# A hybrid decoder layer on one core: attention interleaved without emptying points, deeper load leads, later area returns, block sums ahead

## The chip, the cores and the metric

The kernel runs on one core of a Trainium2 chip. The metric is the device time of one execution in microseconds (us). Engines: PE is TensorE (matrix products), DVE is VectorE, ACT is ScalarE, POOL is GpSimd, and SP is the engine that here only issues DMAs. All engines share the on-chip memory and synchronise by semaphores; each works through its own instructions strictly in order.

## The reference, cut to what matters

One layer of a decoder with 512 positions and model width 2048. Two attentions read columns of one input projection, two sigmoid gates from the same projection weigh them, then come a cross attention to 256 memory tokens and an MLP. All in float32.

```python
def reference(x, mem, g_mix, w_in, ...):
    xn = rmsnorm(h, g_mix[l])
    (q_a, k_c, v_c, k_s, v_s, k_w, v_w, g_nsa, c_q, c_kv, k_r,
     gate_a, gate_b) = jnp.split(xn @ w_in[l], bounds, axis=-1)
    ...
    o_a = nsa_attention(q_a, kc, vc, ks, vs, kw, vw, g_nsa, ...)
    o_b = mla_attention(c_q, c_kv, k_r, mla_g_q[l], mla_w_uq[l], mla_g_kv[l],
                        mla_w_uk[l], mla_w_uv[l], cos_b, sin_b)
    mixed = (jax.nn.sigmoid(gate_a) * (o_a @ w_o_nsa[l])
             + jax.nn.sigmoid(gate_b) * (o_b @ w_o_mla[l]))
    h = h + mixed @ w_out[l]
    h = h + memory_cross_attention(rmsnorm(h, g_xattn[l]), rmsnorm(mem, g_mem[l]),
                                   xa_wq[l], xa_wkv[l], xa_wo[l])
    hn = rmsnorm(h, g_mlp[l])
    h = h + jnp.square(jax.nn.relu(hn @ w_ff1[l])) @ w_ff2[l]
return rmsnorm(h, g_final)
```

NSA has 16 heads of width 96 with three branches (compressed, selected, window); MLA has 16 heads, whose queries come from a latent of rank 512 (`w_uq`), and keys and values from one of rank 256 (`w_uk`, `w_uv`).

## The kernel before, in words

**Values.** Every float32 operand is held as a high part and a low remainder, `HL`. A product takes three matmuls (`mm`, L513 to L515: high by high, high by low, low by high). The split costs an ACT copy (`hr`, L526, L335, L1789, L1865) and a DVE subtraction (`lr`, L527, L347, L1794, L1870).

**Stages.** The program is a chain of projections, in this order: P0 to P6 (the input projection's columns for NSA), M0 and M1 (`proj_m`: columns for MLA's latents and `w_o`'s input), mk0, mk1, mv (`mem_k`, `mem_v`: the memory's keys and values), then `mla()`: uq (`mla_q`, MLA's queries, four heads for each q of 0 to 3), ukv (`mla_kv`, keys and values of the same heads), mk2 and mk3, and wn (`wn`, four column blocks of `w_o_nsa`). Then g0 to g3 (`Gates.run`: both gates' columns in four blocks, each in 7 products of a Strassen-like scheme, so 28 passes), wm (`w_o_mla`), `w_out`, the cross attention and the MLP. Up to wn most go through `chunk`, which calls `on_k(k)` and one step of the generator `bg` at each k step.

**Attention beside.** Attention doesn't have stages of its own. `Side` holds a queue of generators. After each product of a stage `side.run(rate / 4, ...)` emits so many attention steps: score matmuls (L513 to L515 into `st`), a softmax with DVE maximum and ACT exponential (L701, L702) and DVE scaling (L720), transposes of the probabilities (L799), their ACT and DVE splits (L543, L544) and the product with the values (L818, L820). The rates stand in the table `T`, by stage: r0 to r2 for P and M, rk for mk and mv, ru for uq, rw for ukv and wn, rt for the gates. A stage's `post` generator, also run beside later stages, transposes its heads (`heads_T`, L648); q's and K's heads are first turned by the rope, on POOL (`rope`, L632 to L635). `side.drain()` runs the queue empty at one place. It is called at the end of mv (all of NSA), after mk3, and after ukv1, ukv2 and ukv3 (MLA's heads of one q each).

**What sets the order.** All orders are written out by hand: an instruction stands in its engine's queue where the program emits it. There is no scheduler.

**Memory.** On-chip memory is a pool of 40 areas of 128x1024 words (`slots`, printed `s`) and five pairs (`d`); `get` takes an area and `put` gives it back. Whoever takes a returned area waits, on the chip, until its last reader is done.

**Weights.** `Stream` and, in the gates, `load`, `high`, `low` (`prep`) bring them: SP issues plain loads, POOL issues loads that add to an area (L1784). `prep(i)` runs AHEAD = 3 steps before the product.

**Blocks written to memory and read again.** NSA's and MLA's output goes block by block to `d_nsa` and `d_mla`; `load_o` reads it back and splits it (L526). It holds two halves of areas: it issues block j, then splits block j − 1. `mem_load` does the same for the memory's 16 half blocks in M1, two per k from k = 5. `Gates.fetch` loads x (`xT`, 16 blocks of 256 KB on SP) and multiplies each block by its gain on ACT (L2215, two instructions for each), two k steps per k of wn3, into the eight areas `A`.

**Block sums.** Of a column block's 7 products, n = 1 to 4 multiply a sum of A's blocks. `stat` makes the sum on POOL (`add`, L1838 to L1844) and its high part on ACT (L1865), `stat_low` the low one on DVE (L1870); for c = 0 in the pass before its use, later blocks use it again. `use` takes a finished product: into a sum area for n < 3; from n = 3 on it ends one output block: ACT's Tanh (L2306), a DVE product with the NSA branch for the first two column blocks (L2311), a store to `d_g` by ACT's queue (L2313), and `put`.

## Time and profile before

| | us |
|---|---|
| median of 3 runs | 2884.34 (2883.65 to 2887.16) |
| the profiled execution's own time | 2884.04 |
| its span in the trace | 2882.2 |
| mean granted TensorE clock | 0.988 of full speed |

The stages, by the first matmul of each in the trace (us from the start of the span):

| stage | start | stage | start | stage | start |
|---|---|---|---|---|---|
| P6 | 341.3 | mk3 | 652.2 | wn2 | 794.8 |
| M0 | 412.9 | uq1 | 660.0 | ukv3 | 828.7 |
| M1 | 475.8 | wn0 | 676.6 | wn3 | 843.2 |
| mk0 | 554.3 | ukv1 | 712.9 | g0 | 886.0 |
| mv | 574.7 | uq2 | 722.8 | g1 | 1000.4 |
| uq0 | 619.3 | wn1 | 734.8 | g2 | 1092.2 |
| mk2 | 635.3 | ukv2 | 768.7 | g3 | 1168.4 |
| ukv0 | 646.6 | uq3 | 782.8 | wm | 1254.0 |

How to read the profile's rows: `635.32 0.58 PE L513 MATMUL mm<-s,s ... [7.56 <-ACT s L1284]` is an instruction that started at 635.32 us and took 0.58, of line 513 on PE; it writes a tile of the name `mm` and reads two areas `s`; the engine had stood idle for 7.56 us, and what ended that was ACT's instruction of line 1284 on an area. A row of the waits, `ACT s L1789 <- DMA d_g<-s: 23.5, 6, 9.2`, is an instruction group, what it waited for, the us in total, the number of waits and the longest. A row of the windows gives a stretch of time, its length, each engine's busy time with the number of instructions, the granted TensorE clock, the mean busy share of the DMA engines and GB/s.

### The profile page before, as it was taken

Reading aid. Unit: us, or ns where it says so; the run is one execution under the profiler, and the core shown is the slowest. Engines: PE = TensorE matmul, PEld = TensorE weight load, DVE = VectorE, ACT = ScalarE, POOL = GpSimd, SP = SyncE. Lnnn points to the kernel's source line nnn. Section 1 sums busy time; section 2 is a strip of 40 time slices with the busy share of each in tenths; the row PEclk is TensorE's granted clock in tenths of the full one; section 3 lists DMA queues with packets and bytes.
Section 4 is the critical chain, followed back from the end, with each engine's and each line's share of the span. In section 5 each row is a group of like instructions: output and inputs, shape, how many; then the busy total and the mean of one; then the engine's idle time right before and its main releaser. Section 6 shows DMA issues by size and latency. Waiting matters only on the chain.

```text
span 2882.2 us, 38227 instructions
## 1 busy us (share of the span) xinstructions
PE 2794.2 (97%) x13974; PEld 2365.4 (82%) x13974; DVE 2020.2 (70%) x3179; ACT 1648.9 (57%) x2746; POOL 483.7 (17%) x698
## 2 busy tenths in 40 slices
PE   9999999889987989999999999999999999999998
PEld 7888889878876768778998888888888888888887
DVE  6347677766655667645786677777776788888888
ACT  5445556656665556643465866666666654444445
POOL 3130110111112211100230111111111111111110
PEclk9999999999998999999999999999999999999999
DMA  5322112233236888867862799888898889999996
GB/s 180 97 87 67 57 63 68 80 106 99 78 120 161 231 207 210 213 213 217 185 140 81 214 240 220 205 218 211 211 219 206 208 229 227 233 236 231 241 226 175
DMA packets 165357, 497.95 MB, mean 173 GB/s; under 512 B 17072, under 2 KB 34352, under 8 KB 165168
## 3 DMA queue, kind: packets, MB, share of 16 engines
q0 software_dynamic: 50688, 184.57, 34.1%
q1 hardware_dynamic: 85088, 271.44, 27.6%
q10 hardware_dynamic: 29392, 39.50, 3.9%
q8 instruction: 109, 1.79, 0.3%
q14 instruction: 80, 0.66, 0.1%
HBM read 453.50 MB, written 41.94 MB: 172 GB/s over the span
## 4 chain that ended last, share of the span: by engine, by line
PE 57%; DMA 3%; DVE 3%; issue 3%; ACT 1%; POOL 1%; ACTq 0%; DVEq 0%; POOLq 0%; SPq 0%
PE mm L1976 9%; PE mm L1977 9%; PE mm L1975 9%; PE st L1977 5%; PE st L1975 5%; PE st L1976 5%; PE mm L513 2%; PE mm L514 2%; PE mm L515 2%; DMA d_g<-s 1%; PE mm L1565 1%; PE mm L1563 1%; PE mm L1564 1%; DVE s L1794 1%; PE mm L2053 1%
## 5 line engine op out<-in xcount | busy, mean ns | idle before, releaser
L1975 PE MATMUL mm<-s,s 128*128 128x512 f32 x1472 | 579.7, 394 | 13.6 <-ACT s L1789 10.7
L1976 PE MATMUL mm<-s,s 128*128 128x512 f32 x1472 | 577.9, 393 | 7.7 <-DVE s L1794 7.7
L1977 PE MATMUL mm<-s,s 128*128 128x512 f32 x1472 | 577.6, 392 | 3.2 <-DVE s L1870 3.2
L1794 DVE TENSOR_TENSOR s<-s,s 128x1024 fp32r<-128x1024 f32 x316 | 383.3, 1221 | 201.8 <-ACT s L1789 196.4
L1789 ACT CAST s<-s 128x1024 fp32r<-128x1024 f32 x316 | 327.2, 1049 | 184.7 <-DMA s<-wts 129.0
L513 PE MATMUL mm<-s,s 128*128 128x512 f32 (+5 forms) x1012 | 400.4, 396 | 13.9 <-ACT s L1284 11.8
L515 PE MATMUL mm<-s,s 128*128 128x512 f32 (+5 forms) x1012 | 384.0, 379 | 0.7 <-DVE s L530 0.6
L514 PE MATMUL mm<-s,s 128*128 128x512 f32 (+5 forms) x1012 | 383.3, 379 | 0.0
L347 DVE TENSOR_TENSOR s<-s,s 128x512 fp32r<-128x512 f32 (+4 forms) x408 | 284.1, 714 | 81.8 <-ACT s L335 81.3
L1975 PEld LDWEIGHTS mm<-s,s 128*128 128x128 f32 x1472 | 279.3, 190 | 71.8 <-ACT s L1789 11.9
L1976 PEld LDWEIGHTS mm<-s,s 128*128 128x128 f32 x1472 | 279.0, 190 | 67.5 <-DVE s L1794 10.9
L1977 PEld LDWEIGHTS mm<-s,s 128*128 128x128 f32 x1472 | 279.0, 190 | 63.5 <-DVE s L1870 5.5
L335 ACT CAST s<-s 128x512 fp32r<-128x512 f32 (+4 forms) x408 | 241.4, 604 | 147.8 <-PE mm L515 44.5
L1784 POOL DMA_DIRECT2D s<-wts x167 | 145.9, 875 | 734.2 <-DVE s L1794 420.3
L1975 PE MATMUL st<-s,s 128*128 128x512 f32 x676 | 264.2, 391 | 0.0
L1977 PE MATMUL st<-s,s 128*128 128x512 f32 x676 | 262.8, 389 | 0.0
L1976 PE MATMUL st<-s,s 128*128 128x512 f32 x676 | 262.5, 388 | 0.0
L1789 ACT CAST s<-d 128x1024 fp32r<-128x1024 f32 x159 | 165.1, 1048 | 167.3 <-DMA d<-wts 155.4
L1794 DVE TENSOR_TENSOR s<-d,s 128x1024 fp32r<-128x1024 f32 x159 | 193.2, 1220 | 53.9 <-ACT s L1789 53.0
L513 PEld LDWEIGHTS mm<-s,s 128*128 128x128 f32 x1012 | 192.5, 190 | 39.0 <-ACT s L1284 12.4
L515 PEld LDWEIGHTS mm<-s,s 128*128 128x128 f32 x1012 | 192.0, 190 | 34.3 <-DVE s L530 2.0
L702 ACT ACTIVATE PP<-PP,mx 128x512 f32<-128x512 f32 (+2 forms) x208 | 116.1, 558 | 171.1 <-DVE mx L701 170.3
(399 smaller groups left out, 5152.2 us busy)
## 6 DMA issues: line engine op xcount, KB each, us to landing
s<-wts SPq DMA_DIRECT2D x280, 512.0 KB, 4.9
s<-wts POOLq DMA_DIRECT2D x199, 512.0 KB, 8.3
d<-wts POOLq DMA_DIRECT2D x101, 512.0 KB, 8.6
d<-wts SPq DMA_DIRECT2D x58, 512.0 KB, 7.5
PP<-wts POOLq DMA_DIRECT2D x52, 512.0 KB, 8.6
PP<-wts SPq DMA_DIRECT2D x33, 512.0 KB, 8.4
d_u<-s ACTq DMA_DIRECT2D x64, 256.0 KB, 5.3
s<-xT SPq DMA_DIRECT2D x47, 256.0 KB, 4.1
```

Of the source, the lines that this page charges most:

```text
L335: self.k.nc.scalar.copy(o.hr, self.at[n][:, s])
L347: self.k.nc.vector.tensor_sub(o.lr, t[:, s], o.hi)
L513: t.matmul(ps, a.hr, b.hr, start=first, stop=False)
L514: t.matmul(ps, a.hr, b.lr, start=False, stop=False)
L515: t.matmul(ps, a.lr, b.hr, start=False, stop=last)
L702: self.later("x", 1, lambda: nc.scalar.activation(p, p, AF.Exp, bias=mx, scale=-1.0, accum_out=sm))
L1784: self.nc.gpsimd.dma_start(t, src, accum_op=OP.add)
L1789: self.nc.scalar.copy(t.hr, self.raw[i])
L1794: self.nc.vector.tensor_sub(t.lr, r, t.hi)
L1975: m(ps, a.hr, b.hr, start=first, stop=False, skip_group_check=True)
L1976: m(ps, a.hr, b.lr, start=False, stop=False, skip_group_check=True)
L1977: m(ps, a.lr, b.hr, start=False, stop=last, skip_group_check=True)
```

## The change

It has five parts.

1. `mla()` no longer drains. Attention's generators are put into the queue when their heads are ready (by ukv's `post`), and run on through the stages until they are done, within the gates. The order of the stages becomes uq(q), ukv(q), wn(q − 1). `d_nsa` is read back in uq1 and ukv1 and no longer in uq0 and uq1. The rates change to match, with rv for ukv0 and r3 for uq1 and ukv1 added.
2. `load_o` has four halves, and loads three steps ahead of the split; it waits until a block's store has been emitted. `mem_load` has the same lead, and runs one half block per k through all of M1.
3. `fetch` loads x by eight DMAs of 512 KB, straight into `A`, and POOL multiplies in place by the gain.
4. `presum(n)` makes the sum of n on POOL a pass earlier than `stat` did; `stat` only splits it.
5. `use` doesn't give the area of a `d_g` store back at once but after the next pass's products (`done`).

TensorE's attention and head-transposing instructions beside each stage, by the order of the program before and of the changed one:

| | M0 | M1 | mv | uq0 | mk2 | ukv0 | mk3 | uq1 | wn0 | ukv1 | uq2 | wn1 | ukv2 | uq3 | wn2 | ukv3 | wn3 | g0 |
|---|---|---|---|---|---|---|---|---|---|---|---|---|---|---|---|---|---|---|
| before | 192 | 188 | 117 | 0 | 16 | 0 | 18 | 18 | 93 | 23 | 26 | 83 | 43 | 26 | 83 | 43 | 69 | 69 |
| changed | 149 | 150 | 115 | 18 | 43 | 14 | 37 | 21 | 97 | 25 | 27 | 97 | 30 | 27 | 97 | 28 | 85 | 50 |

The core of the diff:

```diff
-T = dict(pace=0.75, r0=3.7, r1=4.05, r2=4.0, rk=1.1, ru=2.6, rw=3.4, rt=0.8)
+T = dict(pace=0.75, r0=3.7, r1=4.05, r2=3.0, rk=1.15, ru=2.9, rv=3.7, r3=2.6, rw=3.9, rt=0.9)
...
         def on_k(k):
             if k:
                 self.put(self.X[k - 1])
-            if k > 4:
-                for _ in range(2):
-                    next(ml, None)
+            next(ml, None)
...
     def mla_kv(self, q, qs, rate):
...
-        self.side.post = self.heads_T(4, out.append)
-        return out, vs
+        def post():
+            yield from self.heads_T(4, out.append)
+            self.side.add(self.attend(self.mla_items(q, qs, out, vs)))
+            if q == 3:
+                self.side.add(self.flush())
+        self.side.post = post()
...
     def mla(self):
...
-        self.side.drain()
...
+        qs = self.mla_q(0, T["ru"])
+        self.mem_k(2, T["rk"])
+        self.mla_kv(0, qs, T["rv"])
+        self.mem_k(3, T["rk"])
...
-            if q < 3:
-                self.wn(q, T["rw"])
-                ks, vs = self.mla_kv(q + 1, T["rw"])
-                self.side.drain()
+        self.bg = self.load_o(self.d_nsa, self.N)
+        for q in range(1, 4):
+            qs = self.mla_q(q, T["ru"] if q > 1 else T["r3"])
+            self.mla_kv(q, qs, T["rw"] if q > 1 else T["r3"])
+            if q == 1:
+                drain(self.bg)
+                self.bg = None
+            elif q == 2:
+                self.mem_scale()
+            self.wn(q - 1, T["rw"])
...
+    def load_o(self, dram, out, lag=3):
+        while len(self.slots.free) < 2:
             yield
+        st, sl = self.halves(4)
+        for j in range(8 + lag):
+            if j < 8:
+                while (id(dram), j) not in self.stored:
+                    yield
+                self.nc.sync.dma_start(st[j % 4], dram[j])
+            if j >= lag:
+                while not self.slots.free:
+                    yield
+                out.append(self.slot_hl())
+                self.split(out[-1], st[(j - lag) % 4])
+            yield
...
     def fetch(self):
...
+                self.A[t, h] = [k.slots.plain() for _ in range(2)]
+                for i in range(2):
+                    d = 8 * h + 4 * i
+                    nc.sync.dma_start(self.A[t, h][i].rearrange("p (k n) -> p k n", k=4),
+                                      k.a["xT"][d:d + 4, :, 256 * t:256 * t + 256].rearrange("k p n -> p k n"))
+        for h in range(2):
+            for t in range(2):
+                yield
+                for i in range(2):
+                    d = G_MIX + 8 * h + 4 * i
+                    x = self.A[t, h][i].rearrange("p (k n) -> p k n", k=4)
+                    nc.gpsimd.tensor_mul(x, x, k.gains[:, d:d + 4][:, :, None].to_broadcast([128, 4, 256]))
+        self.presum(1)
+
+    def presum(self, n):
+        if n > 4:
+            return
+        self.m = self.sums.get(n - 1)
+        self.sums[n] = [self.k.slots.plain() for _ in range(2)]
+        for h in range(2):
+            self.add(n, h, self.sums[n][h])
...
     def run(self, rate):
...
             self.before(c, n)
+            if p < 4:
+                self.presum(p + 2)
...
-            self.use(c, n, ps)
+            while self.done and self.done[0][0] < p:
+                k.put(self.done.popleft()[1])
+            self.use(p, c, n, ps)
...
         nc.scalar.dma_start(self.rows(self.k.d_g, blk, c), o.rearrange("p (t n) -> p t n", t=2))
-        self.k.put(o)
+        self.done.append((p, o))
```

The same in three engines' orders. The first is TensorE's queue in ukv2, where `mm<-s_99` and `mm<-s_97` are ukv's products, L648 or L649 the head transposes into `st`, and L799 or L800 attention's transposes. Before, in the drain behind ukv2:

```order
L515 MATMUL mm<-s_99,d_5423 128x512
L648 MATMUL st<-cst,s_153 96x128 x2
L648 MATMUL st<-cst,s_154 96x128 x2
L799 MATMUL st<-cst,PP 128x128 x4
L818 MATMUL o<-s_1687,d_6825 128x128
```

Changed, in the middle of ukv2:

```order
L516 MATMUL mm<-s_97,s_5223 128x512
L800 MATMUL st<-cst,PP 128x128 x3
L649 MATMUL st<-cst,s_153 96x128 x2
L649 MATMUL st<-cst,s_154 96x128 x2
L514 MATMUL mm<-s_97,s_5248 128x512
```

The pair of L648 or L649 rows stands four times in a row in both (it is shown once). Before they were K's heads of ukv2 behind its last product; now they are the queries of uq2, between ukv2's products, and K's heads follow in wn.

The second is POOL's queue from wn3 to the first gate products: L1307 copies MLA's rope columns, L1784 or L1793 are the loads of weights that add, L2233 the multiplications by the gain, and the L1838 to L1840 or L1847 to L1849 the block sums. Before:

```order
L1307 COPY s_154<-s_154 128x4x32 x2
L1784 DMA s_8393<-wts 128x1024
L1784 DMA s_8395<-wts 128x1024
L1784 DMA s_8404<-wts 128x1024
L1784 DMA s_8406<-wts 128x1024
L1838 TENSOR_TENSOR s_8488<-d_8115,d_8117 128x1024
L1784 DMA s_8393<-wts 128x1024
L1784 DMA s_8395<-wts 128x1024
L1838 TENSOR_TENSOR s_8489<-d_8115,d_8117 128x1024
```

Changed:

```order
L1307 COPY s_154<-s_154 128x4x32 x2
L2233 TENSOR_TENSOR s_8139<-s_8139,gains 128x1024
L2233 TENSOR_TENSOR s_8140<-s_8140,gains 128x1024
L2233 TENSOR_TENSOR s_8143<-s_8143,gains 128x1024
L2233 TENSOR_TENSOR s_8144<-s_8144,gains 128x1024
L2233 TENSOR_TENSOR d_8125<-d_8125,gains 128x1024 x2
L2233 TENSOR_TENSOR d_8126<-d_8126,gains 128x1024 x2
L1847 TENSOR_TENSOR s_8327<-s_8143,d_8126 128x1024
L1847 TENSOR_TENSOR s_8328<-s_8144,d_8126 128x1024
L1793 DMA s_8360<-wts 128x1024
L1793 DMA s_8362<-wts 128x1024
L1849 TENSOR_TENSOR s_8486<-s_8327,s_8139 128x1024
```

Eight multiplications and the first sum's two halves now stand ahead of the first adding load.

The third is ACT's queue in the first gate block, behind an output block's store. Names are areas with their uses numbered: L1789 or L1798 takes weights' high parts, L1865 or L1877 the sums'. Before:

```order
L2313 DMA d_g_89<-s26_8875 128x2x512
L1789 CAST s9_8965<-d4_8771 128x1024
L1865 CAST s10_8971<-d1_8116 128x1024
L1789 CAST s26_8986<-PP_105 128x1024
L1789 CAST s8_9004<-PP_105 128x1024
```

Changed:

```order
L2346 DMA d_g_89<-s3_8763 128x2x512
L1798 CAST s16_9018<-s32_8360 128x1024
L1877 CAST s8_9023<-d0_8126 128x1024
L1798 CAST s34_9038<-s33_8362 128x1024
L1798 CAST s12_9057<-d1_8127 128x1024
L1877 CAST s28_9063<-d0_8126 128x1024
L1798 CAST s38_9078<-d1_8127 128x1024
L2339 ACTIVATE s36_8667<-s36_8667,hrx_8128 128x512 x2
L2346 DMA d_g_89<-s36_8667 128x2x512
L1798 CAST s6_9103<-s15_9042 128x1024
L1877 CAST s14_9108<-s24_8139 128x1024
L1798 CAST s3_9123<-s31_9061 128x1024
```

Before, the third row behind the store writes into the area that the store reads (`s26`); now it is the eleventh (`s3`), a pass later.

## The prediction, made before the changed kernel was run

> **What bounds the kernel now.** I read the busy shares and the chain of waits of the page first.

> ```profile
> PE 2794.2 (97%) x13974; PEld 2365.4 (82%) x13974; DVE 2020.2 (70%) x3179; ACT 1648.9 (57%) x2746; POOL 483.7 (17%) x698
> PE 57%; DMA 3%; DVE 3%; issue 3%; ACT 1%; POOL 1%; ACTq 0%; DVEq 0%; POOLq 0%; SPq 0%
> ```

> TensorE is busy for 97% of the 2882.2 us span and holds 57% of the chain; no other engine is near its limit over the whole. The change adds and removes practically no matmul, so it can only win where TensorE stands still or runs at a lower granted clock. The next view cuts the span by stage (the table ahead of this prediction names them) and asks each stretch for busy time and granted clock.

> ```profile
> core 0: us, PE busy (x) PEld busy (x) DVE busy (x) ACT busy (x) POOL busy (x), PEclk, DMA share, GB/s
> 412.90:475.80 62.90, 61.61 (x386) 58.27 (x385) 47.51 (x159) 37.52 (x108) 9.69 (x32) 1.00 0.20 61
> 475.80:554.30 78.50, 69.74 (x381) 62.44 (x379) 57.20 (x180) 52.30 (x157) 11.53 (x15) 0.93 0.25 78
> 574.70:619.30 44.60, 41.40 (x216) 33.09 (x215) 32.65 (x95) 25.30 (x67) 0.00 (x0) 1.00 0.34 106
> 619.30:646.60 27.30, 18.12 (x113) 17.36 (x112) 10.40 (x20) 11.71 (x21) 7.14 (x16) 0.87 0.36 126
> 660.00:676.60 16.60, 12.05 (x69) 10.96 (x67) 10.31 (x27) 11.67 (x26) 0.00 (x0) 1.00 0.42 140
> 676.60:712.90 36.30, 36.30 (x189) 30.93 (x190) 24.98 (x66) 20.41 (x48) 8.45 (x20) 0.95 0.20 63
> 734.80:768.70 33.90, 33.90 (x180) 28.70 (x180) 21.04 (x55) 17.83 (x43) 6.99 (x19) 1.00 0.22 70
> 768.70:782.80 14.10, 12.28 (x68) 9.36 (x68) 8.72 (x25) 10.26 (x25) 0.00 (x0) 1.00 0.36 113
> 828.70:843.20 14.50, 12.36 (x69) 9.40 (x68) 9.16 (x25) 10.58 (x25) 0.00 (x0) 1.00 0.39 110
> 843.20:886.00 42.80, 34.43 (x166) 28.02 (x164) 22.19 (x60) 30.64 (x72) 1.01 (x1) 0.95 0.57 179
> 886.00:1000.40 114.40, 97.24 (x405) 78.48 (x406) 71.42 (x88) 56.41 (x79) 33.15 (x24) 0.88 0.80 206
> 1000.40:1092.20 91.80, 81.44 (x337) 64.49 (x336) 59.19 (x54) 52.58 (x60) 13.97 (x17) 0.94 0.83 212
> 1092.20:1168.40 76.20, 76.20 (x338) 63.07 (x337) 57.02 (x52) 51.08 (x58) 15.75 (x19) 1.00 0.86 198
> 1168.40:1254.00 85.60, 79.41 (x337) 63.84 (x336) 53.40 (x54) 50.55 (x62) 11.19 (x13) 0.98 0.84 212
> ```

> I call **loss** a stage's length less its PE busy time, plus length times the missing clock. For g0: 114.4 − 97.24 + 0.12 × 114.4 = 30.9 us. So worked out, the others are M0 1.3, M1 14.3, mv 3.2, uq0 with mk2 12.7, uq1 4.6, wn0 1.8, ukv2 1.8, ukv3 2.1, wn3 10.5, g1 15.9, g3 7.9; wn1 and g2 lose nothing. The sum is 107 us: removing every loss would give 2884.04 − 107 = 2777 us. The gates g0 to g3 hold 54.7 of it. The table of waits and single rows of the timeline tell what these losses are made of.

> ```profile
> ACT s L1789 <- DMA d_g<-s: 23.5, 6, 9.2
> POOL s L1784 <- DVE s L1794: 152.5, 18, 52.8
> ACT s L1865 <- POOL s L1838: 7.0, 2, 4.2
> ACT s L526 <- DMA s<-d_mla: 14.5, 5, 5.4
> 635.32 0.58 PE L513 MATMUL mm<-s,s 128*128 128x256 f32 x1 [7.56 <-ACT s L1284]
> 779.50 0.64 PE L648 MATMUL st<-cst,s 128*96 128x128 f32 x4 [0.52 <-DVE s L544]
> 849.85 0.51 ACT L2215 ACTIVATE s<-s,gains 128x256 f32<-128x256 f32 x1 [5.35 <-DMA s<-xT]
> 854.47 0.58 PE L513 MATMUL st<-s,s 96*128 96x256 f32 x1 [5.11 <-DVE s L544]
> 895.48 1.04 ACT L1865 CAST s<-s 128x1024 fp32r<-128x1024 f32 x1 [4.19 <-POOL s L1838]
> 898.14 0.48 PE L513 MATMUL st<-s,s 96*128 96x128 f32 x1 [4.77 <-DVE s L544]
> 976.80 1.99 ACT L1789 CAST s<-PP 128x1024 fp32r<-128x1024 f32 x2 [8.56 <-DMA d_g<-s]
> 977.90 0.79 PE L1975 MATMUL mm<-s,s 128*128 128x512 f32 x1 [4.59 <-ACT s L1789]
> 1068.31 1.04 ACT L1789 CAST s<-s 128x1024 fp32r<-128x1024 f32 x1 [9.25 <-DMA d_g<-s]
> ```

> A bracket holds the idle time before the row, and what ended it. Everywhere the same pattern: ScalarE stands at the head of its order before something that has only just been started (an area that a store is still reading, a load issued a moment ago, a sum that GpSimd is still making), and TensorE behind it runs dry some microseconds later.

> **The change part by part.** All terms are against the profiled execution's own 2884.04 us, of which 2882.2 is span; the median of the runs, 2884.34, is 0.3 us from it, so that no correction is needed.

> *M0 and M1.* TensorE's attention matmuls beside them fall from 192 and 188 to 149 and 150, and the memory's blocks are converted one step per k and not two, three blocks behind their loads. M0 lost 1.3 us with 192, so density alone doesn't stall; M1's loss comes with the doubled ACT work (52.3 us against 37.5). Of 15.6 I take **10**, bounds 4 and 14.

> *mv, uq0 and mk2.* The drain at the end of mv goes, and the 7.56 us before mk2 (ACT converting d_nsa blocks straight after their loads) has attention beside it, with d_nsa moved away. The square root's chain stays. Of 15.9 I take **10**, bounds 4 and 14.

> *uq1 and wn0.* uq1 waited for evacuations behind d_nsa's second half, now spread over uq1 and ukv1. Of 6.4 I take **3.4**, bounds 0 and 6.

> *ukv1 to ukv3.* A drain after each goes (at most 5 us with ukv1), and a wait comes. q's head transposes stood at the end of wn; now they stand in the middle of ukv right behind uq, and need GpSimd's rope, which runs then.

> ```profile
> 794.19 0.49 POOL L632 TENSOR_TENSOR rp<-s,cst 128x128 f32<-128x128 f32 x1 [26.99 <-ACT s L1284]
> 800.21 0.79 POOL L635 TENSOR_TENSOR s<-rp,rp 128x128 f32<-128x128 f32 x1
> ```

> From first to last rope it is 6.8 us, ending 6.2 us after uq3's end at 794.8. ukv's matmuls ahead of the transposes cover some 4 us. At 2 us for each of three places against 5 gained: **−1**, bounds −14 (three waits of 6.2 and the 5) and +5. Behind a waiting transpose stand ukv's own matmuls, on which K's heads wait.

> *wn3 and the fetch.* x's 16 loads of 256 KB and 32 ACT activations become 8 loads of 512 KB and 8 GpSimd multiplies of 128x1024 plus two sums. ACT's 5.35 us wait and the 5.11 us of TensorE that followed go. GpSimd's price comes from the sums of the same shape:

> ```profile
> 892.76 2.69 POOL L1838 TENSOR_TENSOR s<-d,d 128x1024 f32<-128x1024 f32 x1
> 903.31 0.29 DVE L720 TENSOR_SCALAR PP<-PP,r 128x128 f32<-128x128 f32 x1
> 922.83 2.99 DVE L720 TENSOR_SCALAR PP<-PP,r 128x128 f32<-128x128 f32 x1
> 923.08 2.64 POOL L1842 TENSOR_TENSOR s<-s,d 128x1024 f32<-128x1024 f32 x1
> ```

> Ten times 2.69 is 26.9 us of GpSimd, beside weights' loads that it also issues. And it isn't free to VectorE: a 128x128 scaling that elsewhere takes 0.29 us took 2.99 at 922.83 and ended with GpSimd's sum. [...] By the rows, VectorE is busy 22.2 us in 42.8 here, so most instructions find a gap between two of GpSimd's. I take **+2.5** of 10.5; bounds −16.4 (all 26.9 on the path in place of 10.5) and +8.

> *g0 and g1.* Two edits. The area of a d_g store goes back a pass later, so ACT no longer writes into one being read: that wait was 8.56 us before 976.80 and 9.25 before 1068.31, with 4.59 of TensorE idle behind the first. And GpSimd's sums are made a pass ahead: 4.19 before 895.48, 4.77 of TensorE. Of g0's 30.9 I give the stores 8.5 and the sums 18.6 at 60%, 11, less 4 that transfers take back: **15.5**, bounds 5 and 27. Of g1's 15.9, 14 is stores; less 6 taken back: **8**, bounds −8 and 15. What is late next is the loads:

> ```profile
> DMA packets 25468, 76.25 MB, mean 207 GB/s; under 512 B 2423, under 2 KB 2423, under 8 KB 25449
> 1050.00:1060.00 10.00, 8.42 (x37) 6.45 (x36) 7.78 (x8) 6.28 (x7) 2.62 (x3) 1.00 1.07 263
> 1110.00:1130.00 20.00, 20.00 (x90) 16.57 (x89) 15.27 (x14) 15.63 (x18) 4.34 (x5) 1.00 0.65 127
> ```

> The gates' 368 us move 76.25 MB. Shorter by 30, they need 226 GB/s; 263 has been reached with the engines full.

> *g3.* d_mla's blocks come three steps ahead of their conversion (ACT waited 14.5 us in five): **6** of 7.9, bounds 0 and 7.9.

> *Denser attention* in wn1, wn2 and wn3 (97, 97, 85 matmuls against 83, 83, 69): wn0 had 93 and its only loss was the half clock after an earlier idle. **−2**, bounds −6 and 0.

> Sum: 10 + 10 + 3.4 − 1 + 2.5 + 15.5 + 8 + 6 − 2 = **52.4**, so 2884.04 − 52.4 = 2831.6, say **2832 us**.

> **The rivals.**
> - *GpSimd holds VectorE.* wn3 takes the lower bound, 18.9 us worse than my term: 2851 us. For it speaks the scaling's 2.99 us, against it that VectorE needs 22.2 us of 42.8 and gets its turn between two multiplies.
> - *The gates become bound by transfers.* If the mean of 207 GB/s is what this mix of loads and stores allows, their 368 us stay, and 29.5 us of the sum fall away: 2861 us. Against it: 263 GB/s at 1050.
> - *Slower: areas held a pass longer starve the loads.* GpSimd's accumulating loads already waited 152.5 us for areas (the L1784 row), and while they did the rate fell to 127 GB/s (1110 to 1130). If the store's area, kept for a pass, and the early sums' two hold g0 and g1 at 127, their 114.4 × 206 + 91.8 × 212 = 43.0 MB take 339 us and not 206: +133, against 28.9 us gained elsewhere: 2988 us. It turns slower than before from 43.0 MB / (206.2 + 28.9) = 183 GB/s downwards. Against it: wn3's early loads and one area in 50 (40 and five pairs) are little.
> - *Everything listed goes.* All upper bounds: 14 + 14 + 6 + 5 + 8 + 27 + 15 + 7.9 = 96.9: 2787 us.
> - *The change doesn't do what it says*: the drains' waits come back at the next evacuation, and stores and sums are waited for a pass later. Then 2884 within 6.

> **How the numbers follow.** Chances: forecast (2815 to 2840) 0.5; GpSimd holds VectorE 0.13; transfer-bound gates 0.13; everything goes 0.14; does nothing 0.04; starved loads 0.06. The range takes in forecast and the first two whole, and the upper half of "everything goes": 2800 to 2864. A measurement of this kernel can tell about 0.2%, 6 us, from no change: faster 0.9, same 0.04, slower 0.06.

> **What would show it.** In the changed profile: no idle of over 3 us ahead of mk2; no ACT wait on d_g's stores in g0 to g3; no ACT wait on GpSimd's sums; ACT's fetch rows gone from wn3, and VectorE rows of 2 to 3 us beside GpSimd's multiplies if the first rival holds. New waits of q's head transposes for the rope, of about 2 us, in ukv1 to ukv3. If the gates show over 225 GB/s and no idle, the second and third rivals fall; if ACT waits for weights with the rate at 207, the second holds; if GpSimd's loads wait for areas for much over 150 us at some 130 GB/s, the third. I am wrong altogether if M1, mk2 and g0 are as long as before.

## The result and the profile after

| | before | changed |
|---|---|---|
| median, us (4 runs each) | 2884.73 (2883.65 to 2887.16) | 2842.51 (2840.89 to 2845.25) |
| span of the profiled execution, us | 2882.2 | 2839.1 |
| mean granted clock | 0.988 | 0.994 |

The ratio is 0.9853, with a 95% interval of 0.9836 to 0.9871: 42 us faster, where 52 were forecast. The page of the changed kernel shows TensorE busier and holding far more of the chain of waits; GpSimd and "issue" have nearly left it, and VectorE and ScalarE hold somewhat more of it.

```profile
PE 2777.9 (98%) x13974; PEld 2359.9 (83%) x13974; DVE 2036.4 (72%) x3179; ACT 1636.9 (58%) x2714; POOL 500.3 (18%) x706
PE 84%; DVE 6%; ACT 5%; DMA 3%; issue 1%; POOL 0%; ACTq 0%; SPq 0%; DVEq 0%; POOLq 0%
```

The windows by stage, cut at the same places in the program as before; the order is now M0, M1, mk0 with mk1, mv, uq0 with mk2, uq1, ukv1, wn0, ukv2, wn1, ukv3, wn3, g0, g1, g2, g3. The columns are those of the prediction's table.

```profile
411.90:466.80 54.90, 54.90 (x342) 52.92 (x341) 38.40 (x130) 31.64 (x90) 9.50 (x32) 1.00 0.22 65
466.80:528.70 61.90, 58.64 (x344) 54.52 (x342) 46.41 (x137) 42.78 (x128) 9.23 (x12) 1.00 0.32 99
528.70:556.30 27.60, 21.80 (x161) 20.22 (x161) 20.13 (x54) 18.66 (x53) 8.00 (x24) 1.00 0.30 86
556.30:599.00 42.70, 40.27 (x215) 34.24 (x213) 32.67 (x105) 26.41 (x78) 0.00 (x0) 0.96 0.33 99
599.00:626.40 27.40, 24.13 (x159) 22.22 (x158) 19.39 (x59) 20.59 (x50) 7.86 (x20) 1.00 0.24 78
644.60:657.20 12.60, 11.96 (x72) 11.09 (x70) 8.58 (x25) 7.65 (x19) 0.00 (x0) 1.00 0.55 187
657.20:671.80 14.60, 10.55 (x49) 8.38 (x50) 8.68 (x17) 8.93 (x20) 8.80 (x20) 0.88 0.30 91
671.80:712.20 40.40, 37.38 (x194) 31.41 (x194) 27.95 (x75) 22.11 (x53) 0.00 (x0) 0.96 0.20 63
725.00:737.30 12.30, 9.85 (x56) 8.13 (x56) 7.87 (x17) 8.70 (x21) 7.44 (x20) 1.00 0.21 67
737.30:773.00 35.70, 35.70 (x197) 30.49 (x196) 25.59 (x70) 20.28 (x50) 0.00 (x0) 1.00 0.20 64
785.70:798.70 13.00, 11.07 (x55) 9.23 (x54) 7.87 (x17) 8.70 (x21) 7.49 (x20) 0.87 0.21 69
834.20:877.10 42.90, 36.98 (x183) 29.57 (x182) 32.15 (x63) 21.09 (x47) 21.89 (x11) 0.96 0.64 199
877.10:974.80 97.70, 87.55 (x386) 71.86 (x387) 78.33 (x80) 58.86 (x76) 29.51 (x24) 0.95 0.92 245
974.80:1051.00 76.20, 76.20 (x338) 63.09 (x337) 55.55 (x51) 47.70 (x54) 12.76 (x15) 1.00 0.92 239
1051.00:1128.70 77.70, 76.95 (x338) 62.88 (x336) 56.15 (x53) 51.39 (x59) 15.49 (x18) 1.00 0.84 200
1128.70:1210.90 82.20, 78.88 (x337) 63.94 (x336) 54.53 (x56) 50.50 (x62) 11.60 (x14) 0.98 0.85 211
```

Worked out as in the prediction, the losses that were 107 us in sum are now about 62: g0's 30.9 has halved, at 245 GB/s, and g1's 15.9 has gone altogether, at 239. But there are new ones: 5.8 in mk0 and mk1 (which lost nothing before), and in ukv1 to ukv3 5.8, 2.5 and 3.6 (before 1.0, 1.8 and 2.1). And wn3 has kept 7.6. The table of waits names part of what is left:

```profile
ACT s L1798 <- DMA d_n<-s: 6.1, 1, 6.1
ACT s L1798 <- DMA d_g<-d: 3.1, 1, 3.1
ACT s L527 <- DMA s<-d_mla: 2.7, 1, 2.7
PE st L649 <- POOL s L636: 8.7, 5, 1.9
```

ACT's waits for d_g's stores have fallen from 23.5 us to 3.1 and those for d_mla's blocks from 14.5 to 2.7. Two are new: TensorE on the rope (L636), and ACT on d_n's store.

The timeline rows of wn3 and of g0's beginning show what the new arrangement costs VectorE. L2233 multiplies by the gains, L1849 makes a sum, and L1803 is a weights' subtraction, of 1.2 us elsewhere.

```profile
844.20 7.90 POOL L2233 TENSOR_TENSOR s<-s,gains 128x1024 f32<-128x1024 f32 x4 [48.07 <-DMA s<-xT]
844.26 1.92 DVE L721 TENSOR_SCALAR PP<-PP,r 128x128 f32<-128x128 f32 x1
846.10 2.40 DVE L347 TENSOR_TENSOR s<-s,s 128x512 fp32r<-128x512 f32 x1
857.06 0.33 PE L514 MATMUL st<-s,s 96*128 96x128 f32 x1 [2.34 <-DVE s L545]
877.91 6.23 DVE L1803 TENSOR_TENSOR s<-d,s 128x1024 fp32r<-128x1024 f32 x1
877.97 5.08 POOL L1849 TENSOR_TENSOR s<-s,s 128x1024 f32<-128x1024 f32 x2
886.12 1.04 ACT L1798 CAST s<-d 128x1024 fp32r<-128x1024 f32 x1 [6.09 <-DMA d_n<-s]
891.17 0.90 PE L800 MATMUL st<-cst,PP 128*128 128x128 f32 x3 [7.67 <-DVE mx L702]
```

The scaling at 844.26 took 1.92 us, where one of its shape took 0.29 at 888.53, and ended 0.09 us behind GpSimd's first multiply; L347 took 2.40 for 0.68 at 841.91. The subtraction at 877.91 took 6.23 for 1.23 at 887.20, beside sums of 5.08 together. By "exclusion" and "shut out" these longer times are meant below.

The largest idle that is left, 7.67 us, has two candidates one behind the other: VectorE's subtraction that ended only at 884.1, and ScalarE, which waited until 886.1 for the area of wn3's last store.

### The profile page after: what moved, and what is told of

Read it like the earlier page. It is cut to its first block, busy times and chain, and to the rows that moved or that the text cites. A ratio compares the mean times of both kernels' runs of the same rounds, so it can differ in the third digit from the quotient of the medians.

```text
span 2839.1 us, 38182 instructions
## 1 busy us (share of the span) xinstructions
PE 2777.9 (98%) x13974; PEld 2359.9 (83%) x13974; DVE 2036.4 (72%) x3179; ACT 1636.9 (58%) x2714; POOL 500.3 (18%) x706
## 4 chain that ended last, share of the span: by engine, by line
PE 84%; DVE 6%; ACT 5%; DMA 3%; issue 1%; POOL 0%; ACTq 0%; SPq 0%; DVEq 0%; POOLq 0%
PE mm L1989 10%; PE mm L1987 10%; PE mm L1988 10%; PE mm L514 7%; PE mm L516 7%; PE mm L515 7%; PE st L1989 5%; PE st L1987 5%; PE st L1988 5%; DMA s<-wts 2%; PE st L800 2%; PE mm L1571 1%; PE mm L1569 1%; PE mm L1570 1%; DVE s L1803 1%
## 5 line engine op out<-in xcount | busy, mean ns | idle before, releaser
L1803 DVE TENSOR_TENSOR s<-s,s 128x1024 fp32r<-128x1024 f32 x299 | 367.1, 1234 | 194.1 <-ACT s L1798 192.1
L514 PE MATMUL mm<-s,s 128*128 128x512 f32 (+5 forms) x1044 | 412.9, 396 | 4.4 <-ACT s L1284 1.9
L1798 ACT CAST s<-s 128x1024 fp32r<-128x1024 f32 x299 | 310.2, 1049 | 182.1 <-DMA s<-wts 141.8
L516 PE MATMUL mm<-s,s 128*128 128x512 f32 (+5 forms) x1044 | 395.4, 379 | 0.2 <-DVE s L531 0.2
L515 PE MATMUL mm<-s,s 128*128 128x512 f32 (+5 forms) x1044 | 395.4, 379 | 0.0
L347 DVE TENSOR_TENSOR s<-s,s 128x512 fp32r<-128x512 f32 (+4 forms) x408 | 289.3, 728 | 86.8 <-ACT s L335 86.4
L1798 ACT CAST s<-d 128x1024 fp32r<-128x1024 f32 x175 | 182.0, 1049 | 189.7 <-DMA d<-wts 159.5
L1803 DVE TENSOR_TENSOR s<-d,s 128x1024 fp32r<-128x1024 f32 x175 | 220.4, 1264 | 70.6 <-ACT s L1798 70.3
L1793 POOL DMA_DIRECT2D s<-wts x155 | 136.1, 878 | 670.8 <-DVE s L1803 385.6
```

Source lines behind the costliest of these rows:

```text
L347: self.k.nc.vector.tensor_sub(o.lr, t[:, s], o.hi)
L514: t.matmul(ps, a.hr, b.hr, start=first, stop=False)
L515: t.matmul(ps, a.hr, b.lr, start=False, stop=False)
L516: t.matmul(ps, a.lr, b.hr, start=False, stop=last)
L1793: self.nc.gpsimd.dma_start(t, src, accum_op=OP.add)
L1798: self.nc.scalar.copy(t.hr, self.raw[i])
```

## The experiments

Each started from the changed kernel, with one edit unless said otherwise. Stage lengths in us are taken from the first matmul of each stage, in the one profiled execution of each run; where nothing is changed in or ahead of a stage they mostly repeat within half a microsecond (mv, wn0 and ukv2 within two, and wn3 once not, as shown below), which is why they tell more than the whole time. The ratio is to the kernel before as it ran beside each group of experiments, with medians of 2884.6 to 2887.4 us.

| run | median | ratio to before (95%) | wn3 | g0 | g1 | g3 |
|---|---|---|---|---|---|---|
| before | 2884.73 | 1 | 42.8 | 114.4 | 91.8 | 85.6 |
| changed | 2842.51 | 0.9853 (0.9836 to 0.9871) | 42.8 | 97.7 | 76.2 | 82.2 |
| e1_return_at_once | 2854.96 | 0.9896 (0.9881 to 0.9911) | 42.8 | 98.8 | 87.5 | 83.7 |
| e2_sums_in_pass | 2853.05 | 0.9889 (0.9874 to 0.9904) | 42.5 | 106.0 | 79.6 | 83.9 |
| e3_dn_areas_later | 2836.84 | 0.9834 (0.9817 to 0.9850) | 40.1 | 93.8 | 76.9 | 82.6 |
| e4_gain_by_vector | 2843.40 | 0.9861 (0.9846 to 0.9876) | 47.5 | 96.9 | 76.2 | 82.7 |
| e5_one_drain | 2842.71 | 0.9853 (0.9838 to 0.9867) | 35.6 | 98.7 | 76.2 | 83.0 |
| e6_lead_of_one | 2837.88 | 0.9831 (0.9815 to 0.9848) | 42.8 | 97.8 | 76.7 | 80.4 |
| e7_dense_m | 2839.04 | 0.9841 (0.9826 to 0.9855) | 35.8 | 98.6 | 76.2 | 82.5 |
| e8_rope_behind_wn | 2837.02 | 0.9833 (0.9818 to 0.9848) | 42.5 | 98.1 | 76.2 | 82.9 |
| e9_no_gain (one run) | 2836.27 | | 38.4 | 97.7 | 76.2 | 82.9 |
| e10_two_halves | 2847.11 | 0.9868 (0.9854 to 0.9883) | 42.9 | 97.8 | 76.2 | 86.2 |
| e11_vector_sums | 2834.89 | 0.9817 (0.9803 to 0.9831) | 43.0 | 91.7 | 77.1 | 83.1 |
| e12_shifted_step | 2826.45 | 0.9796 (0.9783 to 0.9810) | 39.6 | 90.6 | 78.4 | 82.0 |

### The returned areas

```diff
-        self.done.append((p, o))
+        self.k.put(o)
```

> The changed kernel, but the area of each d_g store is given back at once, as before. Theory (the store that is still reading its area held ScalarE, and so TensorE, in g0 and g1): 2855 to 2868 us, 13 to 25 above the changed kernel; ACT waits for d_g's stores of 15 us or more come back, and g1 is 8 to 16 us longer than its 76.2. Rival (the waits on stores were only where missing weights or sums showed first): within 4 us of the changed kernel, g1 under 79 us.

12 us slower, just under the theory's range, and 11.3 of it in g1. The wait is back, with TensorE behind it (an ACT row and a PE row of the timeline); ScalarE's waits for d_g's stores are 13.1 us in two, where the theory had 15 or more:

```profile
1040.78 1.04 ACT L1798 CAST s<-s 128x1024 fp32r<-128x1024 f32 x1 [9.51 <-DMA d_g<-s]
1041.87 0.80 PE L1987 MATMUL mm<-s,s 128*128 128x512 f32 x1 [6.40 <-ACT s L1798]
```

The theory holds for g1. In g0 the edit is worth 1.1 us, no more than one further stretch of half clock there makes (13.65 us at half clock and not 10.24).

### The sums a pass ahead

```diff
-        self.presum(1)
...
-    def fresh(self, n, h):
-        pass
...
-            if p < 4:
-                self.presum(p + 2)
```

> The changed kernel, but GpSimd's block sums are made in the pass before their use, as before, and not a pass earlier. Theory (ScalarE's wait for a sum of 2.7 us held TensorE in g0): 2849 to 2857 us, g0 6 to 14 us longer than its 97.7, ACT waits for GpSimd's sums of 8 us or more. Rival (the sums were hidden, and g0 got shorter by the returned areas and the thinner attention alone): within 3 us of the changed kernel.

10.5 us slower, 8.3 of it in g0, where one idle of TensorE doubles from 7.67 us (the first row is one of the table of waits, the others of the timeline):

```profile
ACT s L1877 <- POOL d L1847: 7.5, 2, 4.2
889.15 1.99 ACT L1798 CAST s<-s 128x1024 fp32r<-128x1024 f32 x2 [9.89 <-DMA d_n<-s]
895.33 1.04 ACT L1877 CAST s<-d 128x1024 fp32r<-128x1024 f32 x1 [4.19 <-POOL d L1847]
898.49 0.90 PE L800 MATMUL st<-cst,PP 128*128 128x128 f32 x3 [15.73 <-DVE mx L702]
```

So taking part 4 or part 5 back costs some 11 or 12 us, each mostly in one block. But in e2 two waits of ScalarE stand in that idle one behind the other: the one for the sum, 4.19 us, and before it the one for the area of d_n's store, which has grown from 6.09 to 9.89. Each makes about half of the 8 us by which the idle grew; why the store's wait grew was not separated.

### What is left in g0: the store's area, then the exclusion

e3 keeps wn3's two store areas until the first pass is over:

```diff
-        self.put(*sl)
+        if c < 3:
+            self.put(*sl)
+        else:
+            self.dn = sl
...
-        self.late, self.done = self.after(), deque()
+        self.late, self.done = self.after(), deque((-1, t) for t in k.dn)
```

> The changed kernel, but the two areas from which wn3 stores the NSA branch are given back after the gates' first pass. Theory (g0's largest idle of TensorE, 7.67 us, starts with ScalarE's 6.09 us wait for that store's area): 2832 to 2837 us, that idle under 2 us, g0 under 91 us. Rival (the idle comes from VectorE, whose subtraction took 6.23 us beside GpSimd's sums and ended at 884.1 us; ScalarE's wait lies beside it): at most 2.5 us faster, g0 over 95 us.

It gains 5.7 us in the median (the intervals of the two ratios overlap); g0 is 3.9 us shorter, and the two causes come apart. wn3's 40.1 us belongs to another matter, taken up with the multiplies. ScalarE's wait is gone, the idle has fallen from 7.67 to 3.69 us, and what ends it now is VectorE alone, with two subtractions that took 7.37 us beside GpSimd's two sums of 5.08 together (a DVE row, a PE row):

```profile
876.42 7.37 DVE L1806 TENSOR_TENSOR s<-d,s 128x1024 fp32r<-128x1024 f32 x2
885.70 0.55 PE L800 MATMUL st<-cst,PP 128*128 128x128 f32 x3 [3.69 <-DVE mx L702]
```

The store's area made 4.0 us of the idle of 7.67. How much of the rest is VectorE's exclusion is tested by e11, which has e3's edit and e8's order (below) in it:

```diff
     def adder(self):
-        return self.nc.gpsimd
+        return self.nc.vector
```

> The changed kernel with three edits: the areas of wn3's store given back after the first pass (as in e3_dn_areas_later), the order uq(q), wn(q - 2), ukv(q) (as in e8_rope_behind_wn), and the gates' block sums made by VectorE a pass ahead and not by GpSimd. Theory (what was left of g0's idle, 3.69 us, was VectorE shut out for 5.08 us of GpSimd's sums, where two sums of its own take some 2.4 us): that idle under 1.5 us, g0 87 to 92 us, no VectorE subtraction over 2 us in g0; total 2825 to 2832 us. Rival (VectorE is the engine that is late in g0, 72 us busy in 94, and eight more instructions hurt it as much as the exclusion): g0 93 us or more, total 2831 to 2838 us.

g0 falls by 2.1 us more than with e3, to 91.7, in the theory's range. VectorE's two sums take 2.35 us together where GpSimd's took 5.08 (a DVE row and a PE row), and no subtraction over 1.9 us is left in g0, where e3 had three of 6.2, 3.7 and 4.9:

```profile
872.41 2.35 DVE L1854 TENSOR_TENSOR s<-s,s 128x1024 f32<-128x1024 f32 x2
881.83 0.90 PE L800 MATMUL st<-cst,PP 128*128 128x128 f32 x3 [2.68 <-DVE mx L702]
```

The idle is 2.68 us and not under 1.5, and the total is in the rival's range; it is no lower than the gains of e3 and e8 added up. So VectorE's own sums cost much of what the exclusion had: net of them it was worth 1.0 us of the idle and 2.1 of g0.

### The multiplies in wn3

e4 moves them to VectorE; e9 takes out the first line of this diff and puts nothing in its place.

```diff
-                    nc.gpsimd.tensor_mul(x, x, k.gains[:, d:d + 4][:, :, None].to_broadcast([128, 4, 256]))
+                    for j in range(4):
+                        nc.vector.tensor_scalar(x[:, j], x[:, j], k.gains[:, d + j:d + j + 1], None, op0=OP.mult)
```

> The changed kernel, but x's gains are multiplied by VectorE (32 multiplications of 128x256 with a scalar per partition) and not by GpSimd (8 of 128x1024). Theory (wn3's loss of 10 us comes from VectorE and GpSimd excluding each other, 16 us of it for the multiplies): wn3 4 to 7 us shorter than its 42.9, VectorE's rows of 1.9 to 2.4 us there back at 0.3 to 0.7; 2835 to 2839 us. Rival (the denser attention, 85 instructions beside and not 69, makes wn3's loss): wn3 within 2 us of 42.9 or longer by VectorE's extra work of some 11 us.

> The changed kernel without the multiplication of x by its gains for the gates: GpSimd's eight instructions of wn3 are left out, the two sums behind them stay (what the gates compute differs in this). Theory (GpSimd's 16 us of multiplies shut VectorE out, and that makes most of wn3's loss of 10 us): wn3 36 to 39 us instead of 42.9, and no VectorE row of 1.9 us or more before the sums. Rival (the denser attention and the weights' conversions make the loss, as VectorE is busy 32 us in 43): wn3 41 us or more.

Without them wn3 is 38.4 us, 4.4 less than in the changed kernel. On VectorE they make it 47.5: 32 instructions in its own queue cost 9.1 us and GpSimd's eight 4.4, and the theory was wrong that VectorE could take the work.

How much the exclusion cost in wn3 hung on fractions of a microsecond. e3 changes nothing up to wn3's end, and in its trace every engine runs the changed kernel's instructions in the same order, yet its wn3 took 40.1 us and not 42.8. One scaling makes the difference (a DVE row of the changed kernel, then one of e3):

```profile
844.26 1.92 DVE L721 TENSOR_SCALAR PP<-PP,r 128x128 f32<-128x128 f32 x1
845.46 0.29 DVE L721 TENSOR_SCALAR PP<-PP,r 128x128 f32<-128x128 f32 x1
```

In the changed kernel it began 0.06 us behind GpSimd's first multiply and sat it out; in e3 it began 0.13 us ahead of it. Behind its idle of 2.34 us (the row at 857.06 above) the changed kernel then ran at half clock for 3.41 us (its 128x512 products took 0.63 us there and 0.39 behind it), which costs 1.7 of the 2.7 us; e3 had an idle of 2.25 and no half clock (0.40 us each). Of the eight runs with these multiplies and 85 attention instructions in wn3, seven took 42.5 to 43.0 us there, and e3 alone 40.1. So the multiplies' share of wn3's loss is 4.4 us against the usual length, and 1.7 against e3's.

### The emptying point

```diff
         self.mem_v(T["rk"])
+        self.side.drain()
```

> The changed kernel, but with one emptying of the attention put back, at the end of mv. Theory (a drain costs its chain's latency because nothing of the projections stands between its steps): mv with uq0 and mk2 loses 6 to 11 us more than now; 2847 to 2853 us. Rival (what made mk2 wait 7.56 us was the d_nsa blocks converted behind their loads alone, which stay moved): within 3 us of the changed kernel.

The total does not move, though mv, uq0 and mk2 lose 18.3 us in its windows and not 7.4 (the rows are mv, uq0, mk2 and wn3):

```profile
556.20:620.80 64.60, 57.33 (x282) 46.83 (x281) 48.33 (x163) 39.47 (x114) 0.00 (x0) 0.87 0.22 66
620.80:629.30 8.50, 8.50 (x49) 8.47 (x48) 4.22 (x13) 3.74 (x8) 0.69 (x2) 0.98 0.39 125
629.30:639.60 10.30, 7.83 (x66) 7.39 (x65) 3.59 (x6) 4.70 (x9) 6.20 (x16) 1.00 0.30 103
842.90:878.50 35.60, 34.01 (x180) 28.38 (x178) 28.68 (x64) 20.14 (x45) 21.69 (x11) 1.00 0.74 237
```

So 11 us come back, as many as the theory had, but not where the kernel before lost them. 15.7 of the 18.3 lie in mv, whose drain now empties the queue of 183 attention instructions; before the change it was 117, and mv lost 3.2. Behind the drain uq0 again has no attention beside it and loses 0.2 us, and the idle of 7.56 us ahead of mk2 doesn't return. The rival is right about that idle: it was the d_nsa blocks', and their move took it away. The 11 us are then made up: ukv0 to uq1 have less attention left and are 3.8 us shorter, wn0 is 2.5 shorter, and wn3, with the same eight multiplies, takes 35.6 us and not 42.8.

e7_dense_m did the same by another way:

```diff
-r2=3.0
+r2=4.0
```

> The changed kernel, but with the rate of attention beside M0 and M1 at 4.0 as before and not 3.0. Theory (M1's loss of 14 us came from memory blocks converted two per k, not from the density): M0 and M1 grow only by the matmuls that come into them, some 10 to 14 us, and mk0 to wn3 and g0 shrink by as much; within 3 us of the changed kernel. Rival (the density did it): M1 loses 8 us or more again and the total is 2848 us or more.

```profile
411.70:474.60 62.90, 61.61 (x385) 58.24 (x384) 47.50 (x159) 37.50 (x108) 9.70 (x32) 1.00 0.20 61
474.60:554.20 79.60, 69.11 (x382) 61.90 (x380) 53.82 (x177) 50.90 (x153) 9.43 (x13) 0.96 0.24 77
```

M1 (the second row) is 79.6 us again and loses 13.7 (79.6 − 69.11 of PE busy, and 4% of clock), though the memory's blocks come one per k. So spreading the blocks gained next to nothing, and the thinner attention nearly all. But density stalled only where the blocks stood beside it: M0 (the first row) has as much attention and loses 1.3. M0 and M1 together are 25.7 us longer, where the theory had 10 to 14; yet the total is not worse, since mk0, mv, uq0 and wn3 are shorter. In e5 and e7 attention stands one step further at wn3's beginning, with 82 instructions beside wn3 and not 85. e12 makes this shift alone, in e11:

```diff
-        self.wn(2, T["rw"])
+        self.wn(2, 4.0)
```

> e11_vector_sums with one number changed: wn2's attention rate 4.0 and not 3.9, so that wn3 begins one attention step later in the order (three instructions fewer are left for it: 82 and not 85, the same step sequence at its beginning as in e5_one_drain and e7_dense_m, whose wn3 took 35.6 and 35.8 us and not 42.8 with the same multiplies on GpSimd). Theory (how much of GpSimd's 16 us of multiplies reaches TensorE is set by where in attention's cycle of score, softmax and transposes they fall): wn3 35 to 38 us instead of 43.0, wn2 within 2 us of 35.6; total 2826 to 2830 us. Rival (in e5 and e7 wn3 was short because attention further ahead or x's loads stood otherwise, not because of the step): wn3 41 us or more, total within 3 us of e11's 2834.9.

wn3 falls from 43.0 to 39.6 us, half of what e5 and e7 showed, and neither theory's nor rival's range has it. That the step is a cause is likely and not shown: all three runs with it have a shorter wn3 than the eight without, but e12's is only 0.5 us below e3's, which has no step. With 2826.45 us this is the fastest kernel of the study: its interval lies wholly under the changed kernel's.

### Lead, or number of buffers

```diff
-    def load_o(self, dram, out, lag=3):
+    def load_o(self, dram, out, lag=1):
```

> The changed kernel, but load_o loads one step ahead of its conversion and not three (its four half areas stay). Theory (the lead is what took the ACT waits of 14.5 us on d_mla's blocks out of g3, and lets d_nsa's pass beside uq1 and ukv1): g3 3 to 5 us longer than its 82.2, uq1 and ukv1 together 3 to 6 us longer; 2848 to 2853 us. Rival (the steps lie far enough apart in time that one step of lead covers a load of about 6 us): within 2 us of the changed kernel.

g3 is not longer but 1.8 us shorter, and no wait of ACT for d_mla is left: for d_mla the written lead isn't what counts. For d_nsa the theory had more of a point: uq1 and ukv1 together are 3.7 us longer, within its 3 to 6, but wn0 behind them is 4.1 shorter. e10 takes two of the four half areas away as well:

```diff
-        st, sl = self.halves(4)
+        st, sl = self.halves(2)
...
-                self.nc.sync.dma_start(st[j % 4], dram[j])
+                self.nc.sync.dma_start(st[j % 2], dram[j])
...
-                self.split(out[-1], st[(j - lag) % 4])
+                self.split(out[-1], st[(j - lag) % 2])
```

> The changed kernel, but load_o has two half areas and a lead of one, as before the change (with four halves and a lead of one, g3 was not longer). Theory (SP runs ahead of the written order, so that the number of areas sets how early a block is loaded, and not the lead): ACT's waits for d_mla's blocks come back with 10 us or more, and g3 is 2 to 5 us longer than its 82.2. Rival (what shortened g3 lies elsewhere, in the weights' loads or the returned areas): g3 within 1 us of 80.4 to 82.2, waits under 5 us.

```profile
ACT s L527 <- DMA s<-d_mla: 13.2, 4, 5.5
```

The wait is back, and g3 is 86.2 us. e6 and e10 differ in the areas alone. SP does nothing here but issue, and it ran ahead by as many loads as there were areas: the changed kernel's trace has four loads of d_mla issued from 1150.43 to 1151.76 us, the first split of one (L527) at 1161.54 and the fifth load 1.38 us behind it; the trace before has two, at 1190.12 and 1190.50, the first split (L526) at 1193.79 and the third load 1.38 behind.

### The rope

```diff
+            if q > 1:
+                self.wn(q - 2, T["rw"])
             self.mla_kv(q, qs, T["rw"] if q > 1 else T["r3"])
...
-            self.wn(q - 1, T["rw"])
+        self.wn(2, T["rw"])
```

> The changed kernel, but with the order uq(q), wn(q - 2), ukv(q) for q = 2 and 3, so that GpSimd's rope of the queries runs beside a long stage and not beside ukv. Theory (TensorE's waits for the rope are 1.9 us in ukv2 and in ukv3 and cost what they last, with the half clock behind ukv3's): 4 to 7 us faster, 2835 to 2839 us, no wait of TensorE on GpSimd's rope after ukv1. Rival (attention's heads get ready later, so that the queue runs dry in a wn or is left for the gates): same or up to 6 us slower.

5.5 us faster in the median, 4.8 in the span: the waits of ukv2 and ukv3 have gone, while uq2 gets an idle of 3.3 us of its own, behind attention's maximum. The gain is of the expected size; the intervals of the two ratios overlap, and the stages carry the reading.

## Why the prediction was right, and where its steps were not

- **M0 and M1: 10 forecast.** 15.6 us of loss became 3.3, but mk0 and mk1 got 5.8, so 6.5 net. The step that failed is that M1's loss came with the memory's blocks converted two per k: e7 has them one per k, and at the old density M1 loses 13.7 of its 14.3 again. "Density alone doesn't stall" held for M0, which has no blocks beside it.
- **mv, uq0 and mk2: 10 forecast.** 15.9 became 7.4, so 8.5. Of the two reasons given, d_nsa's move is the one that e5 bears out: with the drain back, the idle ahead of mk2 stays away. The drain that went had cost little: mv lost 3.2 with it and loses 4.1 without.
- **uq1 and wn0: 3.4 forecast.** 6.4 became 5.3; what is left is mostly one idle of 3.0 us in wn0 and the half clock behind it.
- **ukv1 to ukv3: −1 forecast, the mis-sized term.** The mechanism was right: the waits for the rope are there, and are 1.9 us at the longest. But 2 us for each of three places was too little: in ukv1 TensorE stops at two heads in a row, 1.9 and 1.6 us, and a half clock follows in ukv1 and ukv3. The three lose 11.9 us where they had lost 4.9, so 7 and not 1.
- **wn3: +2.5 forecast.** 10.5 became 7.6. The fetch's waits went, and GpSimd's multiplies put nearly as much in their place. They are 2.0 us each and not the 2.69 that was carried over from a sum. That all of 26.9 us could be closed to VectorE, the lower bound, no run shows: the eight and the first two sums took 20.9 us, and without the eight wn3 was 4.4 us shorter. "Gets its turn between two multiplies" held in wn3 (L721 and L347, at 1.92 and 2.40 us, wait for about one multiply each); in g0 one subtraction, at 6.23 us, sat out both sums.
- **g0: 15.5 forecast.** 30.9 became 15.0, 15.9 gained; but not by "the stores 8.5": returning the area is worth 1.1 us there (e1), and the sums ahead 8.3 at most (e2). The remaining 6.5 were not separated; g0 also has less attention beside it, 50 instructions and not 69. The 18.6 that the prediction gives to the sums is worked out in none of its lines. So the agreement of this term is in part luck. What is late next was not the loads, as the prediction had it, but the next store in line, d_n's, and VectorE.
- **g1: 8 forecast.** All 15.9 went, 11.3 of it by the returned areas (e1). The 6 us that transfers were to take back didn't show: 239 GB/s in g1 with no idle over 0.3 us. Rivals two and three fall here.
- **g3: 6 forecast.** 7.9 became 5.0, by two more half areas and not by the lead (e6, e10).
- **Denser attention: −2 forecast.** wn1 and wn2 with 97 instructions beside lose nothing.

In sum the gates gave more than forecast and the rest less, which is why the total, 42 us for 52, came out nearer than most terms. Of the rivals, "GpSimd holds VectorE" is real, at 1.7 to 4.4 us in wn3 and, net of VectorE's own sums, some 2 in g0, and so smaller than its 18.9.

## What to carry to other kernels

Look behind every store whose area goes straight back to a pool: here ScalarE, which took the area next, waited for the store (9.51 us in e1 for d_g's, 6.09 in the changed kernel for d_n's), and returning it a pass later gained 12 us net (d_g), and again some 4 in the stage behind (d_n). How early d_mla's loads went out was set by the number of buffers, since SP does nothing else here, and not by how many steps ahead they are written. A wait that goes where a drain goes need not be the drain's: put the drain back and see whether the wait returns. And judge an edit to a hand-written order by its own stage and by the stages behind it, and ask first how far a stage moves by itself: wn3 moved by 2.7 us with its order unchanged.

## What the runs showed of the hardware

The same idle of TensorE cost differently. In the changed kernel both ukv2 and ukv3 had an idle of 1.93 us ahead of a transpose (the first two rows, of the timeline), and only ukv3's was followed by half clock. The stretches at half clock that this trace holds from M0 to g3 begin at 571.06, 666.63, 680.29, 792.93, 857.78, 888.50 and 1192.29 us, all whole multiples of 3.413 us apart; the one at 888.50 lasts 10.24 us, the others 3.41 each. The windows below are cut on that grid: two that share ukv2's idle, then the one that holds all of ukv3's, and the one behind it.

```profile
732.04 0.42 PE L649 MATMUL st<-cst,s 128*96 128x128 f32 x2 [1.93 <-POOL s L636]
792.79 0.56 PE L649 MATMUL st<-cst,s 128*96 128x128 f32 x2 [1.93 <-POOL s L636]
728.08:731.49 3.41, 2.03 (x13) 1.62 (x11) 2.92 (x7) 1.98 (x6) 3.14 (x8) 1.00 0.16 62
731.49:734.90 3.41, 2.34 (x16) 1.99 (x17) 1.88 (x3) 2.02 (x4) 1.22 (x5) 1.00 0.00 0
789.52:792.93 3.41, 1.49 (x10) 1.08 (x10) 2.65 (x7) 1.59 (x4) 2.98 (x7) 1.00 0.02 7
792.93:796.34 3.41, 3.41 (x15) 2.98 (x15) 2.06 (x3) 2.33 (x4) 1.00 (x4) 0.50 0.00 0
```

In the changed kernel a subtraction of 1.2 us took 6.23 beside two of GpSimd's sums, of 5.08 together. A sum that VectorE made itself took half of 2.35 us (e11), one by GpSimd half of 5.08.
